# Staggered starts: each float32r operand of a two-layer encoder trunk begins at another 16-byte offset within 128 bytes

## The chip, the core and the metric

The kernel runs on one core of one Trainium2 chip. The core has a matmul engine (PE in the profile, with its weight loads shown apart as PEld), a vector engine (DVE), a scalar engine (ACT), a general engine (POOL) and a sync engine (SP) that issues most DMAs. The engines run their own instruction streams in order and wait for each other through semaphores. SBUF is the on-chip memory from which the engines read their operands, PSUM the one into which PE accumulates. The metric is the device time of one execution in microseconds, the median of several runs.

## The reference, cut to what matters

Two layers of a streaming encoder run over 256 frames of width 2048. Each layer normalises its input, projects it to about 14400 columns, runs three token mixers side by side (retention, an RG-LRU recurrence, latent attention), projects each back to 2048, gates and adds the three, and applies one output projection. Almost all arithmetic lies in the four large products.

```python
mod = c_act @ ada_w + ada_b                                  # 2048 x 6144, one row
h = rms_norm(x, norm_pre) * (1.0 + scale) + shift
proj = h @ w_in                                              # 256 x 2048 x 14400
y_ret = retention_branch(rq, rk, rv, rg, ret_gn, cos_ret, sin_ret)
y_lru = rglru_branch(lx, lg, lru_conv_w, lru_conv_b, lru_wa, lru_ba, lru_wx, lru_bx, lru_lambda)
y_mla = mla_branch(mq, mkv, mkr, mg, mla_q_norm, mla_w_uq, mla_kv_norm, mla_w_ukv, cos_mla, sin_mla)
merged = (gates[:, :, 0] * (y_ret @ wb_ret)                  # three products of 1024 x 2048
          + gates[:, :, 1] * (y_lru @ wb_lru)
          + gates[:, :, 2] * (y_mla @ wb_mla))
y = merged @ w_out                                           # 2048 x 2048
return x + (1.0 + res_gate) * rms_norm(y, norm_post)
```

Everything is float32, and the tolerance is tight enough that the kernel splits each float32 operand into two parts.

## The kernel before, in words

**Split operands.** PE multiplies in the type float32r, a float32 of fewer bits. Each activation or weight value is split into a high part (a cast to float32r on ACT) and a low part (the value less the high part, on DVE). A product is then three matmuls: high by high, high by low and low by high. For weights this happens in `load_split`: SP loads up to 1 MB into a tile `raw` (line 274), ACT casts it to `wh` (line 297), DVE subtracts to get `wl` (line 298). `wh` and `wl` come from two pools of three buffers each, 128 partitions by 1024 elements. Where two loads are joined into one part, the second one's pieces come from the pool of activation tiles instead.

**Activations.** The class `Act` keeps the split activations in pieces of 128 by 1024 elements (four blocks of 128 rows by 256 frames). The pieces are taken from twelve long-lived float32r tiles; everything else (normalised inputs, gates, results, scratch) is taken from 22 long-lived float32 tiles of the same size. `slot` hands out the tile that has been free the longest, and `release` puts one back at the end of the queue, so who waits for whose last reader depends on how many tiles there are.

**Matmuls.** `gemm_x` (line 355) holds a 128 by 128 block of an activation still and streams 512 columns of weights past it. `gemm_w` (lines 373 to 375) holds a 128 by 128 block of weights still and streams 256 frames of an activation. A small group for the shared rotary key (lines 946 to 948) holds blocks of only 64 columns still. Each matmul instruction comes with its own weight load: it is shown as LDWEIGHTS on PEld and runs beside the matmul ahead of it. The built program has 9888 matmuls with float32r operands, and 564 others in float32.

**Order.** PE and SP run in the order in which the code is written. A layer is a row of groups of matmuls, and generators (`chains`) slip the small work of the mixers between them. DVE, ACT and POOL are ordered by a scheduler, which goes by the dependences, among them the reuse of tiles, and by priorities.

**Start.** At the beginning POOL issues a few small loads: positions, frequencies (line 200, into a scratch tile called `work` in `rope_tables`). ACT and DVE compute the norm of the input (lines 534 to 539, with a scratch tile called `junk`), and DVE begins the sums over `ada_w` (lines 458, 460 and 464), which PE's first transposes (line 476) need.

**Addresses.** In the built program every float32r tile, every `wh`, `wl` and `raw`, and every one of the 22 float32 tiles begins at a multiple of 128 bytes of its partition, and all slices that PE reads from them are steps of 256 bytes or more. So all 9888 float32r matmuls have both operands at offset 0 within 128 bytes. Small tiles lie at other offsets: `junk`, `kd`, `cosr` and `sinr` at 96.

## Time and profile before

| what | value |
|---|---|
| median of 3 runs | 2004.84 us (2002.46 to 2004.97) |
| profiled execution, its own time | 2003.97 us |
| its span, first to last instruction | 2002.2 us |
| mean granted PE clock over the span | 0.988 of full speed |
| PE busy | 1912.2 us (96%), 10684 matmul records |
| DVE busy | 1410.0 us (70%) |
| ACT busy | 984.7 us (49%) |
| HBM traffic | 455.42 MB, 227 GB/s read over the span |

The profiled execution took 2003.97 us by its own measurement, of which 2002.2 us lie between the first and the last instruction; the other 1.8 us lie around them. The page groups instructions by source line and tile names with numbers left out: `float32r` is an activation piece, `wh` and `wl` are weights, `acc` and `mi` are PSUM banks. PE is busy nearly all the time, and a busy PE in this view is not yet a PE at its peak: durations include the pipeline, so the rate of matmuls is read from the starts in the timeline.

### The profile page before, as it was taken

The page shows a single profiled execution, that of the slowest core. Times are in us where ns is not written, and L with a number is a line of the kernel's source. Part 1 is how long each engine was busy: PE and PEld are TensorE (multiplying, and loading weights), DVE is VectorE, ACT ScalarE, POOL GpSimd, SP SyncE. Part 2 cuts the span into 40 slices and gives each one's busy share as a digit, 9 for nine tenths or more (in the row PEclk, how much of TensorE's full clock was granted, in tenths as well). Part 3 has the DMA queues.
Part 4 walks back from the last instruction along what each step waited for, and adds up shares of the span by engine and source line. Part 5 has one row for each costly group of instructions (what it writes and reads, how often), then busy time and mean ns, then how long its engine had stood idle before and what let it go on. Part 6 is the DMA issues. An engine that isn't in the chain of part 4 may idle for free.

```text
span 2002.2 us, 26737 instructions
## 1 busy us (share of the span) xinstructions
PE 1912.2 (96%) x10684; PEld 1668.2 (83%) x10684; DVE 1410.0 (70%) x1782; ACT 984.7 (49%) x1269; POOL 187.9 (9%) x140
## 2 busy tenths in 40 slices
PE   1979999999999999999989999999999999999998
PEld 1868888989988888878879989899998888788886
DVE  7899989897976687867566764446565447686555
ACT  4744548744454445344444674444455444444443
POOL 2233401100000010102010010000000001010110
PEclk9979999999999999999999999999999999999999
DMA  8878873778777777777665545555554657778663
GB/s 260 289 260 291 295 248 134 256 266 290 259 244 251 271 264 256 276 268 247 230 211 183 174 170 190 190 179 190 184 177 145 210 190 250 239 268 275 215 214 126
DMA packets 157053, 457.16 MB, mean 228 GB/s; under 512 B 12224, under 2 KB 20432, under 8 KB 156928
## 3 DMA queue, kind: packets, MB, share of 16 engines
q1 hardware_dynamic: 153248, 443.44, 64.3%
q0 software_dynamic: 3536, 11.75, 2.0%
q8 instruction: 83, 1.36, 0.3%
q14 instruction: 42, 0.34, 0.0%
q10 hardware_dynamic: 144, 0.26, 0.0%
HBM read 451.23 MB, written 4.19 MB: 227 GB/s over the span
## 4 chain that ended last, share of the span: by engine, by line
PE 67%; DVE 17%; DMA 10%; issue 3%; ACT 2%; POOL 0%; DVEq 0%; ACTq 0%; POOLq 0%
PE acc L355 42%; DMA raw<-in_ada_w 9%; DVE float L460 6%; PE acc L374 6%; PE acc L375 6%; PE acc L373 6%; DVE wl L298 6%; DVE float L400 1%; ACT wh L297 1%; DMA raw<-in_w_in 1%; PE mi L719 1%; PE mi L720 1%; DMA float<-in_k_freq 0%; DVE float L774 0%; PE mi L562 0%
## 5 line engine op out<-in xcount | busy, mean ns | idle before, releaser
L298 DVE TENSOR_TENSOR wl<-raw,wh 128x1024 fp32r<-128x1024 f32 (+1 forms) x640 | 794.2, 1245 | 417.8 <-ACT wh L297 415.1
L297 ACT CAST wh<-raw 128x1024 fp32r<-128x1024 f32 (+1 forms) x640 | 665.9, 1042 | 821.1 <-PE acc L355 555.7
L355 PE MATMUL acc<-wh,float32r 128*128 128x512 f32 x3552 | 993.1, 394 | 3.9 <-DVE float L400 3.7
L355 PEld LDWEIGHTS acc<-wh,float32r 128*128 128x128 f32 x3552 | 664.5, 189 | 145.2 <-DVE float L400 6.9
L355 PE MATMUL acc<-wl,float32r 128*128 128x512 f32 x1776 | 560.8, 392 | 13.1 <-DVE wl L298 13.1
L355 PEld LDWEIGHTS acc<-wl,float32r 128*128 128x128 f32 x1776 | 333.4, 188 | 89.1 <-DVE wl L298 19.4
L373 PE MATMUL acc<-float32r,wh 128*128 128x256 f32 x1280 | 367.5, 287 | 4.9 <-ACT float32r L573 4.9
L375 PE MATMUL acc<-float32r,wl 128*128 128x256 f32 x1280 | 365.3, 285 | 1.9 <-DVE wl L298 1.9
L374 PE MATMUL acc<-float32r,wh 128*128 128x256 f32 x1280 | 365.1, 285 | 0.8 <-DVE float32r L574 0.8
L460 DVE SCALAR_TENSOR_TENSOR float<-raw,c_act,float 128x512 f32<-128x512 f32 (+1 forms) x326 | 257.0, 791 | 74.5 <-DMA raw<-in_ada_w 70.3
L373 PEld LDWEIGHTS acc<-float32r,wh 128*128 128x128 f32 x1280 | 248.5, 194 | 6.5 <-ACT float32r L573 5.8
L375 PEld LDWEIGHTS acc<-float32r,wl 128*128 128x128 f32 x1280 | 248.2, 194 | 2.8 <-DVE wl L298 2.7
L374 PEld LDWEIGHTS acc<-float32r,wh 128*128 128x128 f32 x1280 | 248.4, 194 | 1.8 <-DVE float32r L574 1.4
L455 POOL TENSOR_TENSOR float<-float,float 128x512 f32<-128x512 f32 (+1 forms) x49 | 74.6, 1525 | 104.8 <-ACT float L451 99.6
L1050 POOL TENSOR_TENSOR float<-float,float 128x512 f32<-128x512 f32 x32 | 53.7, 1697 | 250.5 <-DVE float L1047 250.5
L400 DVE TENSOR_TENSOR float<-acc,float 128x512 f32<-128x512 f32 x96 | 62.4, 680 | 4.0 <-PE acc L375 2.2
L793 POOL DMA_DIRECT2D float<-in_ret_gn x4 | 2.3, 572 | 569.4 <-PE mi L745 367.0
L476 PE MATMUL mi<-ident,float 128*128 128x128 f32 x64 | 10.6, 304 | 44.5 <-DVE float L464 44.5
L451 ACT ACTIVATE float<-raw,c_act 128x512 f32<-128x512 f32 (+1 forms) x64 | 40.0, 663 | 24.5 <-DMA raw<-in_ada_w 24.3
L476 PEld LDWEIGHTS mi<-ident,float 128*128 128x128 f32 x64 | 8.1, 154 | 46.9 <-DVE float L464 45.7
L404 ACT ACTIVATE float<-acc 128x512 f32<-128x512 f32 x56 | 31.7, 598 | 17.4 <-PE acc L355 16.6
L1047 DVE TENSOR_TENSOR float<-acc,float 128x512 f32<-128x512 f32 x48 | 31.7, 680 | 1.5 <-PE acc L355 1.4
(231 smaller groups left out, 1271.3 us busy)
## 6 DMA issues: line engine op xcount, KB each, us to landing
raw<-in_w_in SPq DMA_DIRECT2D x224, 1024.0 KB, 5.0
raw<-in_ada_w SPq DMA_DIRECT2D x96, 1024.0 KB, 7.0
raw<-in_w_branch SPq DMA_DIRECT2D x48, 1024.0 KB, 6.2
raw<-in_w_out SPq DMA_DIRECT2D x32, 1024.0 KB, 5.4
raw<-in_mla_w_ukv SPq DMA_DIRECT2D x8, 1024.0 KB, 5.5
raw<-in_mla_w_uq SPq DMA_DIRECT2D x8, 768.0 KB, 4.4
float<-in_x SPq DMA_DIRECT2D x8, 512.0 KB, 9.1
float<-in_k_decay POOLq DMA_DIRECT2D x4, 512.0 KB, 4.3
```

Source lines behind the costliest of these rows:

```text
L297: nc.scalar.copy(wh, raw[:, c0:c0 + n])
L298: nc.vector.tensor_tensor(out=wl, in0=raw[:, c0:c0 + n], in1=wh.bitcast(F32), op=ALU.subtract)
L355: mm(b[:, 0:w_n], x, ws[:, j * w_n:(j + 1) * w_n], start=st, stop=sp)
L373: mm(dst, wh[:, cs], act.H(kt), start=first, stop=False, skip_group_check=True)
L374: mm(dst, wh[:, cs], act.L(kt), start=False, stop=False, skip_group_check=True)
L375: mm(dst, wl[:, cs], act.H(kt), start=False, stop=last, skip_group_check=True)
L400: nc.vector.tensor_tensor(out=dst, in0=b, in1=dst, op=ALU.add)
L404: nc.scalar.activation(out=dst, in_=b, func=func)
L451: nc.scalar.activation(out=t, in_=src, func=AF.Copy, scale=c)
L455: nc.gpsimd.tensor_tensor(out=acc[1], in0=acc[1], in1=t, op=ALU.add)
L460: nc.vector.scalar_tensor_tensor(acc[0], src, c, acc[0], ALU.mult, ALU.add)
L1050: nc.gpsimd.tensor_tensor(out=dst, in0=dst, in1=gate[hf][:, cs], op=ALU.add)
```

## The change

All float32r tiles get 32 more elements (128 bytes), and what is used of them begins at a shifted column. The twelve activation tiles begin at element 0, 4, 8, ... 28, 0, 4, 8, 12 for good. A `wh` or `wl` tile gets a new shift each time it is handed out, by a counter that goes on by four elements with each tile and skips one more step after every eight, so that the same buffer does not see the same shift each round. Four elements are 16 bytes. To make room, the float32 tiles go from 22 to 21.

```diff
-NSLOT = {F32: 22, F32R: 12}
+NSLOT = {F32: 21, F32R: 12}
+PAD = 32
...
-    store = {dt: [cpool.tile([P, W1], dt, name=f"{dt.name}_{i}") for i in range(n)] for dt, n in NSLOT.items()}
+
+    store = {F32: [cpool.tile([P, W1], F32, name=f"float32_{i}") for i in range(NSLOT[F32])],
+             F32R: [cpool.tile([P, W1 + PAD], F32R, name=f"float32r_{i}")[:, i * 4 % PAD:i * 4 % PAD + W1] for i in range(NSLOT[F32R])]}
+    turn = [0]
+
+    def shifted(t, n):
+        turn[0] += 1
+        c = (turn[0] + turn[0] * 4 // PAD) * 4 % PAD
+        return t[:, c:c + n]
+
...
-                    wh = whp.tile([P, W1], F32R, tag="wh", name=nm("wh"))[:, 0:n]
-                    wl = wlp.tile([P, W1], F32R, tag="wl", name=nm("wl"))[:, 0:n]
+                    wh = shifted(whp.tile([P, W1 + PAD], F32R, tag="wh", name=nm("wh")), n)
+                    wl = shifted(wlp.tile([P, W1 + PAD], F32R, tag="wl", name=nm("wl")), n)
```

In the built program the stationary operand then stands at offset 0 in 1840 of the 9888 matmuls, at 64 in 1104, at 32 or 96 in 2520 and at an odd multiple of 16 in 4424; the streamed operand is spread in the same way (1736 at offset 0). In 1056 matmuls both operands still begin at the same offset.

PE and SP issue the same instructions in the same order as before. On DVE, ACT and POOL a few rows move, since one float32 tile fewer changes which tile follows on which. New line numbers are 10 higher from `free_full` on.

The first place is the beginning of DVE's stream. L203 multiplies the loaded frequencies by the positions, L248 to L260 compute a softplus table, L539, L413 and L536 belong to the norm of the input. Before:

```order
L192 CAST cosr<-sinr 128x256
L203 TENSOR_SCALAR float_18_94<-float_18_94,pos 128x32 x2
L248 TENSOR_SCALAR s_386<-e_385 128x8
L249 RECIPROCAL s_386<-s_386 128x8
L250 TENSOR_TENSOR s_386<-s_386,e_385 128x8
L251 TENSOR_TENSOR ss_387<-s_386 128x8
L256 TENSOR_SCALAR e_385<-vec_131 128x8
L252 TENSOR_SCALAR q_388<-ss_387 128x8
L254 SCALAR_TENSOR_TENSOR q_388<-q_388,ss_387 128x8 x6
L255 SCALAR_TENSOR_TENSOR q_388<-q_388,s_386 128x8
L257 SCALAR_TENSOR_TENSOR e_385<-q_388,e_385 128x8
L539 TENSOR_TENSOR xtot_148<-xss_145 128x1
```

And now, the rows from the same xtot on (L549 is the old L539, L213 the old L203, L546 the old L536):

```order
L549 TENSOR_TENSOR xtot_147<-xss_144 128x1
L270 TENSOR_SCALAR sp_42_404<-e_384 128x8
L270 TENSOR_SCALAR sp_43_406<-e_384 128x8
L423 RECIPROCAL rstd_5_149<-rstd_5_149 128x1
L213 TENSOR_SCALAR float_4_80<-float_4_80,pos 128x32 x2
L546 SCALAR_TENSOR_TENSOR float_5_81,xss_152<-float_3_79 128x1024
L549 TENSOR_TENSOR xtot_155<-xss_152 128x1
```

The multiplication of the frequencies has moved from ahead of the softplus to behind the first rstd, just ahead of the second half's square.

The second place is the beginning of POOL's stream, where the frequencies are loaded, with the semaphores that each row waits for. Before:

```order
L161 DMA ident<-in_k_ident 128x128
L187 DMA pos_i<-in_positions 128x2x1
L191 DMA sinr<-in_positions 128x256
L195 DMA fcol<-in_k_freq 64x1 x2
L200 DMA float_18_94<-in_k_freq 128x32
L455 ISA
L455 TENSOR_TENSOR float_7_83<-float_7_83 128x256 [waits Activation_49]
```

And now:

```order
L171 DMA ident<-in_k_ident 128x128
L197 DMA pos_i<-in_positions 128x2x1
L201 DMA sinr<-in_positions 128x256
L205 DMA fcol<-in_k_freq 64x1 x2
L210 DMA float_4_80<-in_k_freq 128x32 [waits Activation_49]
L465 ISA
L465 TENSOR_TENSOR float_7_83<-float_7_83 128x256 [waits Activation_49]
```

The load now goes into the tile that the norm used as `junk` (number 4 instead of 18), and waits until ACT has written its last square there.

## Rows read from the trace of the kernel before

**Rows 1.** The page: busy time, share of the span, instructions, by engine.
```profile
PE 1912.2 (96%) x10684; PEld 1668.2 (83%) x10684; DVE 1410.0 (70%) x1782; ACT 984.7 (49%) x1269; POOL 187.9 (9%) x140
```

**Rows 2.** The page: the chain that ended last, by engine.
```profile
PE 67%; DVE 17%; DMA 10%; issue 3%; ACT 2%; POOL 0%; DVEq 0%; ACTq 0%; POOLq 0%
```

**Rows 3.** Busy time by stretch, with columns named in the first line.
```profile
core 0: us, PE busy (x) PEld busy (x) DVE busy (x) ACT busy (x) POOL busy (x), PEclk, DMA share, GB/s
20.00:40.00 20.00, 2.23 (x8) 1.43 (x8) 19.80 (x54) 8.33 (x16) 5.68 (x7) 1.00 0.79 267
...
1300.00:1500.00 200.00, 200.00 (x1369) 186.45 (x1369) 116.96 (x121) 88.05 (x105) 0.00 (x0) 1.00 0.55 182
```

**Rows 4.** Timeline, gemm_x, PE: start us, length us, engine, line, operation, tiles.
```profile
1000.53 0.39 PE L355 MATMUL acc<-wl,float32r 128*128 128x512 f32 x1
...
1005.29 0.39 PE L355 MATMUL acc<-wl,float32r 128*128 128x512 f32 x1
```

**Rows 5.** Timeline, gemm_w, PE.
```profile
1339.87 0.28 PE L373 MATMUL acc<-float32r,wh 128*128 128x256 f32 x1
...
1342.03 0.28 PE L373 MATMUL acc<-float32r,wh 128*128 128x256 f32 x1
```

**Rows 6.** Timeline, rotary key with 64 stationary columns, PE.
```profile
1329.99 0.28 PE L946 MATMUL acc<-float32r,wh 128*64 128x256 f32 x1
...
1332.71 0.28 PE L946 MATMUL acc<-float32r,wh 128*64 128x256 f32 x1
```

**Rows 7.** Groups by line and shape: busy us, mean ns of one, idle before.
```profile
L373 PEld LDWEIGHTS acc<-float32r,wh 128*128 128x128 f32 x1280 | 248.5, 194 | 6.5 <-ACT float32r L573 5.8
L946 PEld LDWEIGHTS acc<-float32r,wh 128*64 128x64 f32 x32 | 4.3, 134 | 0.4 <-ACT wh L297 0.3
```

**Rows 8.** DVE at shifted starts (one line's instructions), and at aligned starts (timeline).
```profile
L862 DVE SCALAR_TENSOR_TENSOR float<-float,vec,float x48: 469/473/2507, 300.1 to 1116.4; 128x255 f32<-128x255 f32 x16, 128x254 f32<-128x254 f32 x16, 128x253 f32<-128x253 f32 x16
...
30.31 0.48 DVE L460 SCALAR_TENSOR_TENSOR float<-raw,c_act,float 128x256 f32<-128x256 f32 x1
```

**Rows 9.** ACT from PSUM: groups writing an aligned tile and junk.
```profile
L404 ACT ACTIVATE float<-acc 128x512 f32<-128x512 f32 x56 | 31.7, 598 | 17.4 <-PE acc L355 16.6
L431 ACT ACTIVATE junk<-acc 128x512 f32<-128x512 f32 x16 | 9.6, 597 | 21.8 <-PE acc L355 21.5
```

**Rows 10.** PE transposes: weight loads from kd and aligned tiles (min/median/max ns).
```profile
L645 PEld LDWEIGHTS mi<-ident,kd x8: 138/140/143, 391.5 to 1357.1; 128*128 128x128 f32 x8
...
L562 PEld LDWEIGHTS mi<-ident,float x64: 138/141/231, 37.3 to 1086.5; 128*128 128x128 f32 x64
```

**Rows 11.** Timeline of the start: POOL, ACT and DVE.
```profile
4.23 0.57 POOL L200 DMA_DIRECT2D float<-in_k_freq  x1
...
10.35 1.06 ACT L534 ACTIVATE float<-float 128x1024 f32<-128x1024 f32 x1 [0.65 <-DMA float<-in_x]
...
10.59 0.29 DVE L192 CAST cosr<-sinr 128x256 f32<-128x256 int32 x1 [2.73 <-DMA sinr<-in_positions]
13.16 0.39 DVE L203 TENSOR_SCALAR float<-float,pos 128x32 f32<-128x32 f32 x2 [2.28 <-DMA float<-in_k_freq]
13.46 0.17 DVE L248 TENSOR_SCALAR s<-e 128x8 f32<-128x8 f32 x1
...
15.99 0.15 DVE L539 TENSOR_TENSOR xtot<-xss 128x1 f32<-128x1 f32 x1
...
17.54 1.23 DVE L536 SCALAR_TENSOR_TENSOR float<-float 128x1024 f32<-128x1024 f32 x1 [0.88 <-ACT float L534]
```

**Rows 12.** DMA issues: KB each, median us from issue to landing.
```profile
float<-in_ret_gn POOLq DMA_DIRECT2D x4, 256.0 KB, 4.0
...
float<-in_k_freq POOLq DMA_DIRECT2D x1, 16.0 KB, 8.8
```

**Rows 13.** Timeline and line: a load on POOL, whom it now follows, its reader.
```profile
622.98 0.55 POOL L795 DMA_DIRECT2D float<-in_k_decay  x1 [38.57 <-DVE float32r L581]
...
655.03 1.23 DVE L581 TENSOR_TENSOR float32r<-float,float32r 128x1024 fp32r<-128x1024 f32 x1 [0.46 <-ACT float32r L580]
...
L803 DVE TENSOR_TENSOR float<-mi,float x12: 681/687/693, 717.8 to 1732.8; 128x512 f32<-128x512 f32 x12
```

## The prediction

> **What bounds the kernel now.** I read the page's busy times first. PE is busy 1912.2 of 2002.2 us, DVE 1410.0, ACT 984.7 [rows 1], and two thirds of the chain that ended last are PE's [rows 2]. The stretches tell where that holds. From 20 to 40 us PE works 2.2 of 20 us while DVE works 19.8; from 1300 to 1500 us PE works all 200 us at a granted clock of 1.00 while DVE works 117 and ACT 88 [rows 3]. So after a start that DVE sets, the kernel goes at the rate at which PE takes matmuls, and a change of that rate by one nanosecond is multiplied by the 9888 float32r matmuls: 9.9 us.
>
> That rate has to be read from starts, not from durations. In gemm_x two matmuls of the same kind that lie seven rounds of three apart start at 1000.53 and 1005.29 us [rows 4]: 4.76 us / 21 = 226.7 ns for 512 streamed columns. In gemm_w eighteen matmuls take 1342.03 - 1339.87 = 2.16 us [rows 5]: 120.0 ns for 256 columns. The difference is 106.7 ns for 256 columns, 0.417 ns per column, which is one cycle of the 2.4 GHz level that a granted clock of 1.00 stands for. Taking the columns off leaves 13.3 ns in both: 32 cycles per matmul that do not depend on how much is streamed. The rotary key group shows what they depend on. With 64 stationary columns instead of 128, twenty-four matmuls take 1332.71 - 1329.99 = 2.72 us [rows 6], 113.3 ns each, which leaves 6.7 ns, 16 cycles. So the stream loses a quarter of a cycle for each stationary column, one cycle for each four float32r values, and four such values are 16 bytes. I read this as one read of 16 bytes for the stationary operand that takes one cycle from the streamed one. Over 9792 matmuls with 128 columns and 96 with 64 the loss is 9792 x 13.3 + 96 x 6.7 ns = 131 us. This is the only thing that different starts of the operands could give back.
>
> **Part 1: different starts on PE.** Nothing before shows float32r matmuls at another start, so the price is bounded from both sides. The gain is at most what is lost now, in those matmuls whose operands no longer begin alike: 9888 - 1056 = 8832, times 13.3 ns, 117 us. The loss is what a wider read would cost, below: at most 26.8 us. I take zero, for three reasons from the rows.
>
> First, the loss is exactly one cycle for each 16 bytes, at 64 and at 128 columns, and for all the pairs of tiles and slices that lie between the rows quoted. If the two reads met only where they fall on the same one of eight places within 128 bytes, a part of them would miss. Second, the two operands are not read at the same pace. A weight load lasts 194 ns for 128 columns and 134 ns for 64 [rows 7], 0.94 ns per column, while the stream takes 0.417 ns per column: over one weight load the stream runs past every place within 128 bytes several times, whatever the starts were. A shift moves the moment at which the two meet, not how often they do. Third, the new starts are all multiples of 16 bytes, so that a weight block is still 32 reads of 16 bytes.
>
> The Trainium skill speaks against a gain here too: "TensorE: Matmul & The Clock Gate", section "Step-by-step: what each phase is for", has PE reading its two operands through two independent ports, so that a weight load takes nothing from a running matmul. By that rule there would be nothing to win, zero where the rows leave room for 117 us, and the second rival below would fall away; the trace does not agree with it in full, since 13.3 and 6.7 ns go with the size of the weight load.
>
> Transposes give the one row with a PE operand off a multiple of 128 bytes: kd lies at 96. Its weight loads take 140 ns against 141 ns for the aligned tiles [rows 10]. They are float32, not float32r, and 96 is a multiple of 32, so this tells only that a start of its own does no harm there.
>
> **Part 2: shifted writes and reads on DVE and ACT.** The casts write `wh`, the subtractions read `wh` and write `wl`, 620 of each at full width. In the convolution of the recurrence the code has DVE write at 4, 8 and 12 bytes past an aligned start (line 862); its median is 473 ns for 253 to 255 columns, against 0.48 us for the aligned 256 columns of line 460 [rows 8]. ACT takes 597 ns to write 512 columns to `junk`, at 96 within 128, and 598 ns to write them to an aligned tile [rows 9]. So zero for both. If it were a few per cent all the same, most of the kernel would hide it, since DVE and ACT have 83 and 112 us to spare in the 200 us after 1300 [rows 3]; only the first 200 us would feel it.
>
> **Part 3: one float32 tile fewer.** PE and SP issue the same rows in the same order. At the start DVE now stands at L192 until 13.16 us because it waits for the frequencies [rows 11], and only then does the softplus, from 13.46, and the sum of the norm at 15.99. In the changed program the softplus comes straight after L192, which ends at 10.88; with the same 2.53 us between the two rows the sum is done 2.6 us earlier. That is the best case. But the load of the frequencies now waits for ACT's second square, whose busy stretch ends at 11.4 us [rows 11], and the multiplication stands ahead of L536. A load on POOL's queue takes 4.0 us when it is alone and took 8.8 us here, behind the others of the start [rows 12]: it lands between 15.4 and 20.2 us. Then L536, now at 17.54, can start at 20.2 + 0.4 = 20.6, or 3.0 us later. So this part is worth -2.6 to +3.0 us at L536, and the end takes over at most that, since later waits can absorb it. I take zero, since 15.4 to 20.2 lies around 17.5.
>
> Further on, several loads on POOL wait longer. The longest such wait in layer 0 is the second decay table: it was issued at 622.98 and now follows the split of the attention output, which ends at 656.3 [rows 13]. What stands right behind it on the queue is another load, and the decay tables are first read at 717.8 [rows 13]: 60 us of cover. No price.
>
> **Sum.** 0 + 0 + 0 on the profiled execution's 2003.97 us. The median of the runs is 2004.84 us, 0.9 us above it, and I forecast that median unchanged: **2004.8 us**. About 0.2%, or 4 us, is what a measurement of this kernel can tell from no change; on PE that is 0.4 ns or one cycle per matmul.
>
> **Rivals.**
>
> *Wider reads, slower.* If the stationary operand is in truth fetched in units of more than 16 bytes, each costing the stream its width in cycles, a block that begins inside a unit needs one unit more. Nothing in rows 4 to 7 tells units of 16 from wider ones, since every block there begins at a multiple of 128 bytes and both sizes are multiples of 256. With units of 32 bytes (2 cycles, 0.83 ns) the 4424 matmuls at odd multiples of 16 pay 3.7 us: 2008.5. With 64 bytes (4 cycles, 1.67 ns) the 8048 less 1104 at offset 64, so 6944, pay 11.6 us: 2016.4. With 128 bytes (8 cycles, 3.33 ns) the 8048 not at offset 0 pay 26.8 us: 2031.6. The side is decided at an average of one cycle per matmul. Against it stands that wider fetches are a poor fit for a loss of just one cycle per four values.
>
> The Trainium skill's "SBUF — State Buffer", section "Specifications (TRN2)", puts SBUF's lines at 16 bytes, with a price for each step to a new line. By that rule the shifted blocks touch as many lines as before, and the price would be zero where the rows leave 3.7 to 26.8 us; the trace agrees as far as one cycle for each 16 bytes goes [rows 5, 6].
>
> *Staggering works, faster.* If the loss of 32 cycles comes from both operands beginning at the same place, the 8832 matmuls that no longer do may lose it: at most 117 us, 1888 us; a tenth of that would be 1993. For it: the loss is real and tied to the weight load. Against it: the two paces of Part 1.
>
> *The start decides.* -2.6 or +3.0 us with nothing else: 2002.2 or 2007.8, both within 4 us. With a small cost of DVE's shifted writes in the DVE-bound start it could pass the upper bound.
>
> That the change doesn't do what it says is ruled out: the offsets of the built program are spread as described.
>
> **How the numbers follow.** No change on PE and a start within its bounds: 0.63. Wider reads 0.17, and 0.05 for a start or DVE and ACT writes that cost more than 4 us: slower 0.22. Staggering works 0.12, and 0.03 for a start that gains over 4 us by what it lets SP load earlier: faster 0.15. The range goes from 1996, a tenth of the gain's bound with the start at its late end (2004.8 - 11.7 + 3.0), to 2019, units of 64 bytes with the late start (2016.4 + 3.0). It leaves out the larger gains and units of 128 bytes, some 0.17 together.
>
> **What would show it.** If the forecast is right, matmuls of gemm_x still start 226.7 ns apart, gemm_w 120.0 and the rotary key 113.3, with no spread between rounds, and lines 297 and 298 keep their mean. Wider reads would show as 120.8, 121.7 or 123.3 ns in part of gemm_w's matmuls, according to the offset of the weights. A gain would show as gaps between 106.7 and 120 ns. At the start, L536's place tells Part 3: before 17.5 us or up to 20.6. The prediction fails if any group of float32r matmuls has changed its pace by half a nanosecond.

## The result, and the profile after

The changed kernel takes 2017.36 us (2015.79 to 2017.64), 1.0064 times the 2004.84 us of before (95% interval 1.0041 to 1.0087). That is 12.5 us more, where no change was forecast. Its profiled execution has a span of 2015.6 us, 13.4 us more, at a mean granted clock of 0.991.

The page's busy times and its chain by engine, to be held against [rows 1, 2]:

```profile
PE 1924.6 (95%) x10684; PEld 1659.1 (82%) x10684; DVE 1412.2 (70%) x1782; ACT 983.4 (49%) x1269; POOL 186.4 (9%) x140
...
PE 72%; DVE 13%; DMA 9%; ACT 3%; issue 2%; POOL 0%; SPq 0%; DVEq 0%; ACTq 0%
```

PE has become 12.4 us busier with the same instructions; DVE, ACT and POOL have hardly moved. So the time went into PE's own rate, the term that the prediction put at zero. The same matmuls as in [rows 4], [rows 5] and [rows 6], in the timeline of the changed kernel (all its lines are ten further down):

```profile
1010.62 0.39 PE L365 MATMUL acc<-wl,float32r 128*128 128x512 f32 x1
...
1015.49 0.39 PE L365 MATMUL acc<-wl,float32r 128*128 128x512 f32 x1
...
1351.85 0.28 PE L383 MATMUL acc<-float32r,wh 128*128 128x256 f32 x1
...
1353.97 0.28 PE L383 MATMUL acc<-float32r,wh 128*128 128x256 f32 x1
...
1342.01 0.28 PE L956 MATMUL acc<-float32r,wh 128*64 128x256 f32 x1
...
1344.78 0.28 PE L956 MATMUL acc<-float32r,wh 128*64 128x256 f32 x1
```

Twenty-one matmuls of gemm_x now take 4.87 us, 231.9 ns each (226.7 before). Eighteen of gemm_w take 2.12 us, 117.8 ns (120.0 before): faster. Twenty-four of the rotary key take 2.77 us, 115.4 ns (113.3).

Below, "the pace" of a kernel is the mean of all intervals between the starts of two successive matmuls of one shape with 128 stationary columns, intervals with a wait in them (over 239 ns for 512 columns, 133 ns for 256) left out; some 5200 and 4170 intervals per kernel. (In g4_move128 below the limit is 245 ns: some 600 of its intervals are 240 or 241 ns long and have no wait in them. With 245 ns for all, no other kernel's mean moves by more than 0.2 ns.) Before: 227.4 ns with a standard deviation of 2.2 for gemm_x's shape, 119.9 with 0.75 for gemm_w's. After: 231.8 with 3.1, and 118.1 with 2.6. So the paces have not only moved, their spread has grown too. Where PE never waits, the intervals of gemm_x repeat a cycle of 226, 227 and 227 ns in the kernel before; in the changed kernel they follow no short cycle, and 98 of 100 lie between 225 and 239 ns.

A view that shows this without any working out is the busy time by stretch, cut at the same two matmuls in every kernel: a stretch of 384 matmuls of gemm_x with the rotary key behind them, and one of gemm_w that follows. PE never waits in either, at a granted clock of 1.00, so the length of the stretch (first number after the colon) is PE's rate. The kernel before, then the changed kernel with the stretch of [rows 3] ahead:

```profile
core 0: us, PE busy (x) PEld busy (x) DVE busy (x) ACT busy (x) POOL busy (x), PEclk, DMA share, GB/s
1240.87:1333.39 92.52, 92.52 (x435) 77.48 (x433) 40.59 (x34) 41.82 (x47) 0.00 (x0) 1.00 0.56 188
1333.39:1380.34 46.95, 46.95 (x393) 46.75 (x391) 21.13 (x25) 19.11 (x21) 0.00 (x0) 1.00 0.54 180
```

```profile
20.00:40.00 20.00, 2.23 (x8) 1.44 (x8) 19.80 (x53) 7.89 (x16) 5.68 (x7) 1.00 0.78 264
1250.77:1345.48 94.71, 94.71 (x434) 77.70 (x433) 40.60 (x34) 41.70 (x47) 0.00 (x0) 1.00 0.54 183
1345.48:1391.66 46.18, 46.18 (x392) 45.98 (x391) 21.09 (x25) 19.12 (x21) 0.00 (x0) 1.00 0.55 183
```

The first stretch is 2.2 us longer, the second 0.8 us shorter, with DVE and ACT as busy as before. The start is as it was: 2.23 us of PE and 19.80 us of DVE from 20 to 40 us.

### The profile page after: what moved, and what is told of

It reads as the page before. It is cut to its first block, busy times and chain, and to the rows that moved or that the text cites. A ratio compares the mean times of both kernels' runs of the same rounds, so it can differ in the third digit from the quotient of the medians.

```text
span 2015.6 us, 26748 instructions
## 1 busy us (share of the span) xinstructions
PE 1924.6 (95%) x10684; PEld 1659.1 (82%) x10684; DVE 1412.2 (70%) x1782; ACT 983.4 (49%) x1269; POOL 186.4 (9%) x140
## 4 chain that ended last, share of the span: by engine, by line
PE 72%; DVE 13%; DMA 9%; ACT 3%; issue 2%; POOL 0%; SPq 0%; DVEq 0%; ACTq 0%
PE acc L365 45%; DMA raw<-in_ada_w 8%; PE acc L384 6%; PE acc L385 6%; PE acc L383 6%; DVE float L470 5%; DVE wl L308 5%; DVE float L410 1%; DMA raw<-in_w_in 1%; ACT wh L307 1%; PE mi L729 1%; PE mi L730 1%; PE acc L670 0%; PE acc L671 0%; PE acc L672 0%
## 5 line engine op out<-in xcount | busy, mean ns | idle before, releaser
L365 PE MATMUL acc<-wh,float32r 128*128 128x512 f32 x3552 | 1007.0, 398 | 3.9 <-DVE float L410 3.7
L365 PE MATMUL acc<-wl,float32r 128*128 128x512 f32 x1776 | 566.5, 395 | 11.6 <-DVE wl L308 11.5
L383 PEld LDWEIGHTS acc<-float32r,wh 128*128 128x128 f32 x1280 | 244.3, 191 | 7.7 <-ACT float32r L583 6.8
L385 PEld LDWEIGHTS acc<-float32r,wl 128*128 128x128 f32 x1280 | 243.8, 190 | 2.9 <-DVE wl L308 2.9
L384 PEld LDWEIGHTS acc<-float32r,wh 128*128 128x128 f32 x1280 | 244.1, 191 | 1.8 <-DVE float32r L584 1.3
L519 POOL DMA_DIRECT2D float<-in_norm_post x8 | 4.4, 556 | 507.6 <-DVE wl L308 339.2
L414 ACT ACTIVATE float<-acc 128x512 f32<-128x512 f32 x56 | 31.7, 598 | 12.6 <-PE acc L365 12.4
```

The costliest lines, as they stand in the source:

```text
L365: mm(b[:, 0:w_n], x, ws[:, j * w_n:(j + 1) * w_n], start=st, stop=sp)
L383: mm(dst, wh[:, cs], act.H(kt), start=first, stop=False, skip_group_check=True)
L384: mm(dst, wh[:, cs], act.L(kt), start=False, stop=False, skip_group_check=True)
L385: mm(dst, wl[:, cs], act.H(kt), start=False, stop=last, skip_group_check=True)
L414: nc.scalar.activation(out=dst, in_=b, func=func)
```

## The experiments

What the change moves is easiest seen in where the tiles lie. In the kernel before, pieces, `wh` and `wl` are 4096 bytes apart and every float32r operand begins at 128 modulo 256 bytes. The change adds 0 to 112 bytes to each start, but its padding also puts the buffers 4224 bytes apart, so that they begin at 0 and at 128 modulo 256 in turn, shifts or not.

**Which part of the change does it?** Four kernels divide the change.

*e1_layout*: the changed kernel with its padding and all shifts zero.

```diff
-F32R: [cpool.tile([P, W1 + PAD], ...)[:, i * 4 % PAD:i * 4 % PAD + W1] for i in ...]
+F32R: [cpool.tile([P, W1 + PAD], ...)[:, 0:W1] for i in ...]
-        c = (turn[0] + turn[0] * 4 // PAD) * 4 % PAD
+        c = 0
```

> The changed kernel with all shifts set to zero: the float32r tiles keep their 128 extra bytes, there are 21 float32 tiles, DVE, ACT and POOL run the changed kernel's rows, but every float32r operand begins at offset 0 again. Mixed-starts theory (the loss comes from operands that begin at different offsets from one matmul to the next): back to the kernel before, 2002 to 2008 us, gemm_x starts 227.4 ns apart on average and gemm_w 119.9. Layout rival (the loss comes from tiles 4224 instead of 4096 bytes apart, or from the missing float32 tile): stays at 2014 to 2018 us, with 231.8 and 118.1 ns if it is the distance of the tiles, or with the old paces and idle PE elsewhere if it is the missing tile.

*e2_weights*: the kernel before, 22 float32 tiles, only `wh` and `wl` padded and shifted. *e3_pieces*: the changed kernel with the shift of `wh` and `wl` zero.

```diff
 # e2_weights, on the kernel before
-                    wh = whp.tile([P, W1], ...)[:, 0:n]
+                    wh = shifted(whp.tile([P, W1 + PAD], ...), n)      # wl alike
 # e3_pieces, on the changed kernel
-        c = (turn[0] + turn[0] * 4 // PAD) * 4 % PAD
+        c = 0
```

> The kernel before, with the turning shift on wh and wl alone; activation pieces stay at offset 0 and there are 22 float32 tiles. In gemm_x the streamed operand then changes its start and the stationary one does not; in gemm_w it is the other way round. Mixed-starts theory: mixing one side is enough, so both paces leave their fixed values, near 231.8 ns in gemm_x and 118.1 in gemm_w, and the time is 2010 to 2018 us. A rival in which only the start of the stationary operand matters: gemm_w changes to about 118 and gemm_x keeps 227.4, some 1998 us. A rival in which only the start of the streamed operand matters: gemm_x 231.8 and gemm_w 119.9, some 2028 us.

> The changed kernel with the shift on the activation pieces alone; wh and wl begin at offset 0. The mirror of the one before: in gemm_x the stationary operand is shifted, in gemm_w the streamed one, each by a fixed amount per piece, so that high and low part differ but the start changes only every few matmuls. Mixed-starts theory: both paces again near 231.8 and 118.1 ns, 2010 to 2018 us. If only the start of the stationary operand matters: gemm_x 231.8, gemm_w 119.9, some 2028 us. If only the streamed one matters: gemm_x 227.4, gemm_w 118.1, some 1998 us.

*e4_sweep*: the kernel before with padded `wh` and `wl` and one shift for a whole group of matmuls, the next multiple of 16 bytes for the next group of its kind.

```diff
+    def begin(mode):                       # called once at the head of gemm_x ("x") and gemm_w ("w")
+        now[0] = groups[mode] * 4 % PAD
+        groups[mode] += 1
-                    wh = whp.tile([P, W1], ...)[:, 0:n]
+                    wh = whp.tile([P, W1 + PAD], ...)[:, now[0]:now[0] + n]      # wl alike
```

> The kernel before, with wh and wl at one shift for a whole group of matmuls and at the next multiple of 16 bytes in the next group of its kind; pieces at offset 0, 22 float32 tiles. Read by group in the trace. Mixed-starts theory: inside a group every matmul meets the same starts as the one ahead, so each group has a narrow spread, and those at offset 0 have 227.4 and 119.9 ns; whether other offsets settle at other paces is open. Fixed-offset rival (some distances between the two starts are dear by themselves, others cheap): paces differ from group to group by offset and repeat when the offset comes round again, with the mean over the eight offsets at 231.8 and 118.1 ns. If no offset matters: 227.4 and 119.9 in all groups and about 2005 us.

All four came out as slow as the change itself:

| kernel | time, us | ratio to before (95% interval) | pace gemm_x, ns | pace gemm_w, ns |
|---|---|---|---|---|
| e1_layout | 2015.33 | 1.0059 (1.0043 to 1.0076) | 231.2 | 118.3 |
| e2_weights | 2015.94 | 1.0062 (1.0044 to 1.0081) | 231.7 | 118.1 |
| e3_pieces | 2018.58 | 1.0078 (1.0054 to 1.0103) | 231.8 | 117.9 |
| e4_sweep | 2016.29 (one run) | | 231.4 | 117.9 |

The two stretches of e1_layout:

```profile
1249.89:1344.32 94.43, 94.43 (x434) 77.61 (x433) 40.60 (x34) 41.68 (x47) 0.00 (x0) 1.00 0.54 184
1344.32:1390.84 46.52, 46.52 (x392) 46.32 (x391) 21.08 (x25) 19.12 (x21) 0.00 (x0) 1.00 0.55 182
```

With no shift at all, the stretches are those of the changed kernel within 0.4 us. So the shifts of 16 bytes are not needed for the loss; and since e2_weights and e4_sweep keep all 22 float32 tiles, the lost tile is not needed either. What all four share is weight buffers 4224 bytes apart. One thing in e4_sweep stood out: the two long groups of gemm_w whose weights were shifted by 64 bytes ran at 113.6 and 113.8 ns (a third one, of 48 matmuls, at 116.1).

**Is it the distance, or where the buffers begin modulo something?** Two kernels pad `wh` and `wl` by 512 and by 256 bytes (21 float32 tiles, no shift), one moves them as a block, one repeats the sweep.

```diff
 # f1_far512 (PAD = 128 values), f3_far256 (PAD = 64), on the kernel before
-                    wh = whp.tile([P, W1], ...)[:, 0:n]
+                    wh = whp.tile([P, W1 + PAD], ...)[:, 0:n]      # wl alike
 # f2_move64: an unused tile ahead of wh and wl, which stay 4096 apart
+    gap = gapp.tile([P, 16], F32, name="gap")
 # f4_sweep512: f1_far512 with one shift per group, as e4_sweep, 0 to 240 bytes
```

> The kernel before with the three wh and three wl buffers 512 bytes longer, so 4608 bytes apart instead of 4096, no shift, one float32 tile fewer (21). Every float32r operand then still begins at 128 modulo 512, as in the kernel before, but the buffers are no longer 4096 apart. Theory A (what slowed the changed kernel is that its buffers begin at different places modulo 512, since they lie 4224 apart): the matmuls of gemm_x keep 227.4 ns from start to start and those of gemm_w 119.9 ns, and the time is 2000 to 2010 us. Theory B (what counts is the distance of 4096 itself, or anything that makes tiles other than 1024 elements): 231 to 232 and 118 ns as in the changed kernel, and 2012 to 2020 us.

> The kernel before with wh and wl 256 bytes longer (4352 apart, starting alternately at 128 and 384 modulo 512), no shift, 21 float32 tiles. Theory A with modulus 512: unsettled paces, between those of before and of the changed kernel or like the latter (gemm_x 229 to 232 ns, gemm_w 118 to 119.5 ns), 2008 to 2018 us. Theory A with modulus 256: 227.4 and 119.9 ns, 2000 to 2010 us. Theory B: 231 to 232 and 118 ns, 2012 to 2020 us.

> The kernel before with an unused tile of 64 bytes ahead of the weight buffers: wh and wl stay 4096 apart, but all begin 64 bytes later against the pieces (at 192 modulo 512 instead of 128). In the sweep, the gemm_w groups whose weights were shifted by 64 bytes ran 113.3 to 114.7 ns apart instead of 118 to 119. Theory A with a fixed relative start (the pace is one fixed number for each fixed relation of the two operands): both paces are settled again, with spreads below 2 ns: gemm_w 112.5 to 115 ns, gemm_x some settled number between 226 and 234 ns. With 3840 matmuls of gemm_w and 5376 of gemm_x the time is 2004.8 - 3840 x 6.2 ns = 1981 us if gemm_x keeps 227.4 ns, and 2004.8 - 23.8 + 5376 x 3 ns = 1997 us if gemm_x goes to 230.4 ns. Theory B (only the distance of the buffers counts): 227.4 and 119.9 ns, 2000 to 2010 us.

> The kernel of f1_far512 (wh and wl 4608 apart, equal places modulo 512, 21 float32 tiles) with one shift for all weights of a group of matmuls: 0, 16, 32 up to 240 bytes, the next value for the next group of its kind. Theory A: within each group the pace is settled (spread below 1.5 ns after the first weights), and it is a function of the shift: 227.4 and 119.9 ns at 0, 112.5 to 115 ns for gemm_w at 64. Theory B, or a cause outside the places of the operands: every group unsettled, 230 to 233 and 117 to 119 ns whatever the shift.

f1_far512: 2005.08 us, ratio 1.0008 (0.9997 to 1.0018), 227.4 and 119.9 ns. f3_far256: 2007.01 us, 1.0013 (0.9999 to 1.0028), 227.4 and 119.9 ns. f2_move64: 1999.85 us, 0.9979 (0.9969 to 0.9988), 229.1 and 114.6 ns. f4_sweep512: 2017.64 us in one run. The two stretches of f3_far256, then of f2_move64:

```profile
1254.68:1347.20 92.52, 92.52 (x435) 77.50 (x433) 40.59 (x34) 41.82 (x47) 0.00 (x0) 1.00 0.57 188
1347.20:1394.15 46.95, 46.95 (x392) 46.75 (x391) 21.12 (x25) 19.10 (x21) 0.00 (x0) 1.00 0.55 180
```

```profile
1236.58:1330.18 93.60, 93.60 (x434) 77.78 (x433) 40.59 (x34) 41.77 (x47) 0.00 (x0) 1.00 0.56 186
1330.18:1375.06 44.88, 44.88 (x392) 44.69 (x391) 20.96 (x25) 19.04 (x21) 0.00 (x0) 1.00 0.58 188
```

Buffers 4352 apart give the lengths of before to a hundredth of a microsecond, so the distance of 4096 is not needed. In f3_far256 the buffers begin at 128 and 384 modulo 512 in turn and the pace does not care: the period is 256 bytes, not the 512 that I had taken. And f2_move64, with every buffer 4096 apart, has other paces because the weights lie 64 bytes further: so the place of the operands sets the pace, and a change of it can win as well as lose. Within the sweep the groups at a shift of 0 ran at 227.8 and 119.8 ns, those of gemm_w at 64 bytes at 113.4, the other shifts at 229 to 235 and 116.7 to 120.0. My expectation that every constant shift gives a spread below 1.5 ns failed: at most shifts the standard deviation within the groups was 1.6 to 5 ns. But that spread is not disorder. Inside a group the intervals repeat a short cycle, in gemm_x for instance 225, 231 and 238 ns at a shift of 112 bytes, and 231 and 236 in turn at 192. A constant shift does settle the pace, into a cycle instead of one interval.

**Undoing it in the changed kernel, and one relation at a time.**

```diff
 # g2_even256: e1_layout with tiles 4352 apart
-PAD = 32
+PAD = 64
 # g3_turn256: the changed kernel with tiles 4352 apart, its shifts of 0 to 112 bytes kept
-PAD = 32
+PAD = 64
-        c = (turn[0] + turn[0] * 4 // PAD) * 4 % PAD
+        c = (turn[0] + turn[0] * 4 // 32) * 4 % 32      # pieces alike
 # g4_move128, on the kernel before
+    gap = gapp.tile([P, 32], F32, name="gap")
```

> The changed kernel with its tiles 256 bytes longer instead of 128 (pieces, wh and wl 4352 apart) and all shifts zero: against e1_layout only the distance changes, from 4224 to 4352. Theory A': every float32r operand begins at the same place modulo 256, so 227.4 and 119.9 ns and 2000 to 2010 us; e1_layout took 2015.3 us with 231.2 and 118.3 ns. Theory B (the padding of the pieces, or another thing that the layout brings): 231 and 118 ns, 2012 to 2020 us.

> The changed kernel with its tiles 4352 apart, and its own turning shifts of 0 to 112 bytes kept: the distance is harmless here, and only the different starts remain. Theory A' (operands at different places modulo 256, by whatever means, unsettle the pace): 231 to 233 and 117.5 to 118.5 ns, 2014 to 2022 us, like the changed kernel. Theory C (the distance did all of it and the shifts of 16 bytes do nothing): 227.4 and 119.9 ns, 2000 to 2010 us.

> The kernel before with an unused tile of 128 bytes ahead of the weight buffers: everything 4096 apart, weights at 0 and pieces at 128 modulo 256, the same relation in every pair. Theory A' with modulus 256: this relation has a pace of its own, as in the sweep's groups at 128 (232.0 and 118.6 ns), so 2004.8 + 5376 x 4.6 ns - 3840 x 1.3 ns = 2024 us at most, 2012 to 2026 us. Theory M (only a mixture of relations disturbs the pace, and 128 is as good as 0): 227.4 and 119.9 ns, 2000 to 2010 us.

g2_even256: 2006.89 us, 1.0011 (1.0000 to 1.0021), 227.3 and 119.9 ns. g3_turn256: 2017.78 us, 1.0066 (1.0049 to 1.0083), 231.5 and 118.2 ns. g4_move128: 2021.18 us, 1.0086 (1.0064 to 1.0108), 232.5 and 119.0 ns. The two stretches of g2_even256, of g3_turn256 and of g4_move128:

```profile
1245.18:1337.69 92.51, 92.51 (x434) 77.47 (x433) 40.60 (x34) 41.82 (x47) 0.00 (x0) 1.00 0.56 188
1337.69:1384.64 46.95, 46.95 (x392) 46.75 (x391) 21.13 (x25) 19.10 (x21) 0.00 (x0) 1.00 0.55 180
```

```profile
1250.42:1344.76 94.34, 94.34 (x435) 77.68 (x433) 40.61 (x34) 41.68 (x47) 0.00 (x0) 1.00 0.55 184
1344.76:1391.03 46.27, 46.27 (x393) 46.06 (x392) 21.08 (x25) 19.11 (x21) 0.00 (x0) 1.00 0.55 183
```

```profile
1250.84:1345.67 94.83, 94.83 (x434) 77.90 (x433) 40.61 (x34) 41.64 (x47) 0.00 (x0) 1.00 0.54 183
1345.67:1392.14 46.47, 46.47 (x392) 46.27 (x391) 21.10 (x25) 19.11 (x21) 0.00 (x0) 1.00 0.56 182
```

128 bytes more per tile bring the layout of the change back to the paces of before. So in e1_layout it was the places modulo 256 and nothing else of the layout. The shifts do the same harm by themselves (g3_turn256). Either half of the change is enough, and the two do not add. And it needs no mixture of relations: in g4_move128 every pair but 48 (where the weights, too, stand in tiles of the activations) has the same one, 128 bytes, and the kernel is as slow.

What a mixture does is not the average of its relations. Set beside the addresses of the built program, some 2500 of e1_layout's intervals in gemm_x begin with a matmul whose two operands lie at the same place modulo 256, and some 2700 with one whose operands lie 128 apart; they last 231.2 and 231.3 ns, not 227.4 and 232.5. In the changed kernel all 16 relations stand at 231.2 to 232.3 ns. So the relation of a matmul's own two operands does not set its interval where its neighbours have another one. By which rule the neighbours act is open.

**One operand against the other, or each by itself?** In the kernels with one relation the weights had so far always been moved against pieces at 128.

```diff
 # h1_both128: an unused tile of 128 bytes ahead of everything
+    lead = cpool.tile([P, 32], F32, name="lead")
 # h2_pieces64: 64 bytes ahead of everything and 192 ahead of wh and wl, which thus keep their place modulo 256
+    lead = cpool.tile([P, 16], F32, name="lead")
+    gap = gapp.tile([P, 48], F32, name="gap")
```

> The kernel before with an unused tile of 128 bytes ahead of everything: pieces and weights all begin at 0 modulo 256 instead of 128, 4096 apart as before; 22 float32 tiles. Theory R (what counts is the place of one operand against the other, modulo 256): 227.4 and 119.9 ns, 92.5 and 46.95 us in the two stretches, 2000 to 2010 us. Theory P (what counts is the place of each operand by itself, and the weights' place at 0 modulo 256 is what slowed g4_move128): 231.4 and 119.0 ns, 94.8 and 46.5 us, 2012 to 2024 us.

> The kernel before with the pieces moved by 64 bytes (to 192 modulo 256) and the weights left at 128, all 4096 apart: the weights lie 192 bytes past the pieces modulo 256. Theory R: the paces of the sweep's groups with a shift of 192, 233.2 ns for gemm_x and 117.8 ns for gemm_w, so 5328 x 5.8 - 3840 x 2.1 ns = 23 us more, 2015 to 2032 us. Theory P with only the weights' place counting: 227.4 and 119.9 ns, 2000 to 2010 us. A theory by which only the distance between the places counts and not which one is ahead: 229.1 and 113.4 to 117.8 ns as in f2_move64, 1995 to 2005 us.

h1_both128: 2004.10 us, 0.9999 (0.9985 to 1.0013), 227.4 and 119.9 ns. h2_pieces64: 2020.89 us, 1.0077 (1.0053 to 1.0101), 233.3 and 117.3 ns. Their two stretches:

```profile
1245.30:1337.81 92.51, 92.51 (x434) 77.47 (x433) 40.59 (x34) 41.81 (x47) 0.00 (x0) 1.00 0.57 188
1337.81:1384.76 46.95, 46.95 (x392) 46.75 (x391) 21.12 (x25) 19.09 (x21) 0.00 (x0) 1.00 0.56 180
```

```profile
1249.55:1344.75 95.20, 95.20 (x434) 77.74 (x433) 40.59 (x34) 41.68 (x47) 0.00 (x0) 1.00 0.55 182
1344.75:1390.03 45.28, 45.28 (x393) 45.08 (x391) 20.96 (x25) 19.03 (x21) 0.00 (x0) 1.00 0.58 187
```

It is the relation. Moving both operands alike changes nothing. Moving the pieces by 64 bytes gives nearly the paces that the sweep had shown where the weights were moved by 192 (233.2 and 117.8 ns): weights 192 bytes past the pieces either way.

**A version faster than both.** gemm_x is best at 0 and gemm_w at 64 bytes, and both use the same weight buffers, so the shift is given with the call: f3_far256 with

```diff
-    def load_split(src, nk, ncol, spare=None):
+    def load_split(src, nk, ncol, spare=None, off=0):
...
-                    wh = whp.tile([P, W1], ...)[:, 0:n]
+                    wh = whp.tile([P, W1 + PAD], ...)[:, off:off + n]      # wl alike
...
-            for k, (wh, wl) in enumerate(load_split(..., nk, W1)):      # in gemm_w
+            for k, (wh, wl) in enumerate(load_split(..., nk, W1, off=16)):
```

> The kernel before with wh and wl 4352 bytes apart (as f3_far256, whose paces were those of before, and 21 float32 tiles), and with the weights of gemm_w alone begun 64 bytes later; those of gemm_x begin where they did. Theory A' (equal places modulo 256 bytes give 227.4 and 119.9 ns; gemm_w's own best place is 64 bytes off, where f2_move64 had a mean of 114.6 ns and the sweep 113.4): gemm_x 227.4 ns, gemm_w 113.4 to 114.6 ns, and 3840 x 5.3 to 6.5 ns = 20 to 25 us less than before: 1979 to 1988 us, faster than both kernels. Rival: gemm_w's gain is lost to its waits for weights or pieces (chain of waits through VectorE and the DMAs), or the change of place between the two kinds disturbs gemm_x as the mixture did: 1995 to 2012 us.

g1_part64 takes 1996.54 us, 0.9961 of before (0.9948 to 0.9974), with 227.4 ns for gemm_x and 115.7 ns for gemm_w. It beats both kernels, by less than half of what I expected. Its two stretches, then the first 415 us and one other group of gemm_w; and behind them the same first part and group in the kernel before:

```profile
1241.09:1333.60 92.51, 92.51 (x434) 77.49 (x433) 40.60 (x34) 41.87 (x47) 0.00 (x0) 1.00 0.56 188
1333.60:1378.06 44.46, 44.46 (x393) 44.26 (x391) 20.97 (x25) 19.06 (x21) 0.00 (x0) 1.00 0.57 190
...
0.00:414.20 414.20, 345.96 (x2263) 310.31 (x2264) 363.62 (x522) 236.41 (x314) 99.14 (x70) 0.98 0.73 255
...
1195.87:1241.09 45.22, 45.22 (x386) 45.22 (x384) 25.84 (x24) 22.40 (x28) 3.23 (x1) 1.00 0.55 187
```

```profile
0.00:415.10 415.10, 352.49 (x2263) 317.82 (x2264) 364.05 (x522) 236.34 (x314) 99.51 (x70) 0.98 0.73 254
...
1194.83:1240.87 46.04, 46.04 (x385) 46.04 (x384) 25.81 (x24) 22.39 (x28) 3.30 (x1) 1.00 0.54 183
```

Two things took most of the rest. First, gemm_w has two levels at this relation: the stretch from 1333.60 runs at 113.4 ns, the group from 1195.87 at 117.8 ns with a standard deviation of 0.6 over 383 intervals, just as steadily. (The 115.7 ns are those of the shape; 480 of its 4320 matmuls do not belong to gemm_w and were left where they were. gemm_w alone is at 115.2.) Interval by interval against the kernel before, gemm_w's matmuls take 17.5 us less. Second, waits take 7.8 us of this back. In the first 415 us PE has 6.5 us less to do, and the stretch is only 0.9 us shorter: there PE stands idle for 68 us anyway, and DVE is busy for 364 of the 414. Waits between 414 and 835 us grow by another 7.5 us, and from 1575.5 us they shrink by 5.3; the other kernels with 21 float32 tiles, too, lose in the stretch from 656 and win in the one from 1575.5 (Part 3 below). Which level a group falls into did not follow from the addresses: some groups ran at one in g1_part64 and at the other in f2_move64, and in f2_move64 the group from 1330.18 even goes from 113.3 to 117.8 ns for 96 matmuls and back. That stays open.

## Why the prediction was wrong, point by point

**Where the bound is: right.** PE's rate of taking matmuls sets the time after the start, and a nanosecond there counts some ten thousand times. By the pace's means the change is 5328 x 4.4 - 3840 x 1.8 ns = 16.5 us for the matmuls of gemm_x and gemm_w, against 13.4 us of span; Part 3 has the difference.

**Part 1, different starts on PE: this step failed.** The term "I take zero" measured +16.5 us, and its reasons do not hold: two are refuted and the third does not bear on the loss. The first was that the loss of 32 cycles was the same "for all the pairs of tiles and slices" between the rows quoted, so that it could not depend on their places. But all those pairs had the same relation modulo 256: tiles lay multiples of 4096 bytes apart, slices multiples of 256. One relation was seen many times, and I took it for many. The second was that the two reads pass each other at different paces, so that the starts would wash out. g4_move128, f2_move64 and h2_pieces64 change nothing but the starts and give 232.5, 229.1 and 233.3 ns for 227.4. The third was that multiples of 16 bytes leave the number of reads alone. That may be so, but the count of reads is not what sets the loss: gemm_w's went from 13.3 ns per matmul to 6.7 at one relation.

The step also looked at the starts only within 128 bytes, which is how the change speaks of them, and passed over what the padding does to the distance of the tiles. With e1_layout it turned out that the padding alone was enough. The measured time lies within the stated range of 1996 to 2019 us by luck. The upper end was the price of wider reads, a mechanism that did not occur. Its bound of 26.8 us holds the net loss of every kernel here but not PE's loss in one product: in h2_pieces64 gemm_x alone lost 5328 x 5.9 ns = 31 us, and gemm_w gave 10 of them back.

The prediction weighed two rules. "TensorE: Matmul & The Clock Gate" of the Trainium skill, section "Step-by-step: what each phase is for", has two independent ports for the operands. h1_both128 against h2_pieces64 does not agree with reads that take nothing from each other: the pace depends on the relation of the two, by up to 5.9 ns. By the line of 16 bytes that the Trainium skill's "SBUF — State Buffer", section "Specifications (TRN2)", gives, these shifts would have no price; the runs do not agree, since h2_pieces64 pays 17 us for 64 bytes. By what means the price arises they do not show.

**Part 2, shifted writes and reads on DVE and ACT: right.** Subtraction and cast in the page of before, then of the changed kernel, the same within 2 ns:

```profile
L298 DVE TENSOR_TENSOR wl<-raw,wh 128x1024 fp32r<-128x1024 f32 (+1 forms) x640 | 794.2, 1245 | 417.8 <-ACT wh L297 415.1
L297 ACT CAST wh<-raw 128x1024 fp32r<-128x1024 f32 (+1 forms) x640 | 665.9, 1042 | 821.1 <-PE acc L355 555.7
...
L308 DVE TENSOR_TENSOR wl<-raw,wh 128x1024 fp32r<-128x1024 f32 (+1 forms) x640 | 795.1, 1246 | 429.1 <-ACT wh L307 427.0
L307 ACT CAST wh<-raw 128x1024 fp32r<-128x1024 f32 (+1 forms) x640 | 664.5, 1040 | 834.0 <-PE acc L365 585.1
```

**Part 3, one float32 tile fewer: right in size, not in every place.** The start in the changed kernel's timeline, to be held against [rows 11]:

```profile
9.79 0.29 DVE L202 CAST cosr<-sinr 128x256 f32<-128x256 int32 x1 [2.64 <-DMA sinr<-in_positions]
9.99 0.17 DVE L258 TENSOR_SCALAR s<-e 128x8 f32<-128x8 f32 x1
...
11.46 0.57 POOL L210 DMA_DIRECT2D float<-in_k_freq  x1 [7.22 <-ACT float L544]
...
12.53 0.15 DVE L549 TENSOR_TENSOR xtot<-xss 128x1 f32<-128x1 f32 x1
...
16.91 0.39 DVE L213 TENSOR_SCALAR float<-float,pos 128x32 f32<-128x32 f32 x2 [3.69 <-DMA float<-in_k_freq]
17.20 1.22 DVE L546 SCALAR_TENSOR_TENSOR float<-float 128x1024 f32<-128x1024 f32 x1
```

The softplus and the sum of the norm come early, the load of the frequencies goes out at 11.46 us behind ACT's second square, and DVE waits for it until 16.91, between the forecast 15.4 and 20.2. L546 begins 0.3 us earlier than L536 did. Taking zero was right.

Further on I had found no price, and there is one that is paid back. Between the same two matmuls (at 655.7 and 831.0 us in the kernel before), before and h1_both128, with 22 tiles, took 175.3 and 174.8 us; f1_far512, f3_far256 and g2_even256, with 21 tiles and the same paces, took 178.7 to 186.7. From 1580.0 to 1750.8 us they took 165.3 to 165.6, before 170.8 and h1_both128 167.4. The slow kernels repeat it: 179.7 to 180.5 us with 21 tiles (the changed kernel, e1_layout, e3_pieces, f4_sweep512, g3_turn256) against 176.7 to 177.7 with 22 (e2_weights, e4_sweep, g4_move128, h2_pieces64), and then 167.4 to 167.8 against 170.5 to 172.6. The whole of f1_far512, f3_far256 and g2_even256 is 0.08 to 0.13% above before, with intervals that reach from -0.03 to 0.28%: at most a few us.

That later stretch is also why the span grew by less than 16.5 us. First in the kernel before, then in the changed kernel, with its first part ahead:

```profile
1580.00:1750.80 170.80, 166.69 (x757) 138.11 (x756) 106.83 (x136) 75.87 (x86) 10.22 (x11) 0.98 0.68 226
```

```profile
0.00:416.50 416.50, 350.59 (x2263) 314.23 (x2264) 365.53 (x522) 236.33 (x314) 97.88 (x70) 0.98 0.73 254
...
1592.00:1759.80 167.80, 167.44 (x756) 136.75 (x755) 105.48 (x133) 75.66 (x86) 9.69 (x10) 1.00 0.68 230
```

From 1580.0 PE stood still for 4.1 us before and for 0.4 after, at a clock of 0.98 and of 1.00, and the stretch became 3.0 us shorter although it holds 672 matmuls of gemm_x, whose intervals became 4.6 ns longer, 3.0 us in all. So waits give back 6 us here. The whole growth can be added up the same way, interval by interval between the same two float32r matmuls of both traces. Intervals without a wait in either kernel add 23.3 us in gemm_x's shape and take 7.2 off in gemm_w's: 16.1 us. Waits take 5.9 us off from 1580.0 on, and add 1.9 us in the first 416 us and 1.8 in the stretch from 655.7; the rest of the kernel takes 0.5 off. 16.1 - 5.9 + 1.9 + 1.8 - 0.5 = 13.4 us, the growth of the span. The waits are those of two single executions; the h1_both128 of above, 3.4 us shorter than before in the same late stretch at the same paces and with as many tiles, tells how far one can differ from another.

**The rivals.** "Wider reads, slower" gave 2016.4 us for units of 64 bytes, 1 us from the result. That is luck, for it is not what happened: it foresaw steps of 120.8 to 123.3 ns in gemm_w according to its offset, where gemm_w became faster, and it could not have slowed e1_layout, whose offsets are all multiples of 128. "Staggering works" holds for gemm_w at one relation and is the reason for g1_part64; as the change does it, mixing all relations, it loses more on gemm_x than it wins on gemm_w. "The start decides" did not.

**What would show it.** The test that I set, "fails if any group of float32r matmuls has changed its pace by half a nanosecond", did its work: both groups had, by +4.4 and -1.8 ns.

## What to carry to other kernels

Where PE runs matmul after matmul, look at where the two operands begin relative to each other, modulo 256 bytes here: padding a tile by other than a multiple of 256 bytes, or allocating a small tile between two pools, can change the matmul's pace, and the relation can be set for each kind of matmul by itself. Read the pace from starts in stretches where PE never waits, and compare the same stretch between kernels: differences of 0.1 us in 92 show there, when whole runs scatter by several. And before a rate is called independent of something, see whether that something varied in the rows at all.

## What the runs showed of the hardware that was not expected

The pace of float32r matmuls, in ns, by how far the weights begin past the pieces modulo 256 bytes, with 128 stationary columns, from the kernels that have a single relation in all but 48 matmuls (standard deviation in brackets):

| weights past pieces | gemm_x: weights streamed, 512 columns | gemm_w: weights stationary, pieces streamed, 256 columns | kernel |
|---|---|---|---|
| 0 | 227.4 (2.2) | 119.9 (0.75) | before |
| 0, both moved by 128 | 227.4 (2.2) | 119.9 (0.83) | h1_both128 |
| 64 | 229.1 (2.6) | 114.6 (2.2), levels of 113.4 and 117.8 | f2_move64 |
| 128 | 232.5 (3.8) | 119.0 (2.5) | g4_move128 |
| 192 | 233.3 (2.1) | 117.3 (1.6) | h2_pieces64 |

Where PE never waits, these paces are fixed cycles: gemm_x repeats 226, 227, 227 ns before, 229, 231 or 232, 226 in f2_move64, and 231, 236 in h2_pieces64; in g4_move128 one interval of 240 or 241 ns follows on every six or seven of 228 to 233. Kernels that mix relations have means of their own (231.2 and 118.3 ns in e1_layout, which has 0 and 128), so this table does not forecast them.

At the 2.4 GHz level the 256 columns of gemm_w last 106.7 ns, so what a matmul with a new stationary block loses beside its stream goes from 13.3 down to 6.7 ns (at the lower level of 64) with the start alone. That the two reads meet in the same memory is my reading of it; no run here shows where.
